# One hybrid decoder layer on one Trainium2 core: preparation behind the masks, fill between sample rounds, the inverse sent in pieces, and z loaded by ScalarE

## The chip, the cores and the metric

The kernel runs on one core of a Trainium2 chip. The metric is the time of one execution on the device in microseconds (us). The core has five engines with an instruction queue each: TensorE (PE, matrix products), VectorE (DVE), ScalarE (ACT), GpSimd (POOL) and SyncE (SP, which issues transfers only). Matrix products land in PSUM, a small memory of banks. SBUF is the large on-chip memory.

## The reference

One layer of a decoder is computed for a prompt of 512 tokens and for 8 sample requests of 4 tokens each, which share the weights; so T = 544 columns go through every product.

```python
def trunk_layer(x, wkv0, shift0, conv0, p):
    x = layer_norm(ALPHA * x + 0.5 * swiglu(x, p["ffn1_wg"], p["ffn1_wu"], p["ffn1_wd"]), ...)
    proj = x @ p["w_in"]
    ...            # r, k, v, decay w, gate a, g from proj with a token shift
    o, wkv_new = wkv7_recurrence(r_h, w_h, k_h, v_h, kk, a_h, wkv0)
    ...            # group norm of o, bonus, gate g
    u = c_c * c_h  # short gated convolution of width 3
    z = cw[0] * u_full[:, 0:T] + cw[1] * u_full[:, 1:T+1] + cw[2] * u_full[:, 2:T+2]
    y_conv = c_b * z
    mix = jnp.concatenate([y_rwkv, y_conv], axis=-1) @ p["w_out"]
    x = layer_norm(ALPHA * x + mix, ...)
    x = layer_norm(ALPHA * x + 0.5 * swiglu(x, p["ffn2_wg"], p["ffn2_wu"], p["ffn2_wd"]), ...)

# wkv7_recurrence, one step per token and head (64 x 64 state S):
    sa = S @ (-kk)
    S = S * w[None, :] + outer(sa, kk * a) + outer(v, k)
    o = S @ r
```

The widths are 1024 for the model, 2816 for the FFN, 8 heads of 64, and 512 channels of convolution. All is in float32.

## The kernel before, in words

**Products.** A float32 product is made of three passes: weights and inputs are split into a high and a low part (`hl`, `xhl`, `hhl`), ACT writing the high part and DVE the low one (`wsplit`), and `mm3` issues high x high, high x low and low x high for each block of 128 x 128. A weight is loaded into a buffer of the ring `raw` by SP, split into one of the ring `hl`, and used. The two FFNs (`Ffn`, `pairs` for gate and up, `downs` for down) use a scheme with fewer block products; `pairs` keeps sums of partial products in `cpb`, `downs` also uses `cpb` as the staging buffer from which a transfer on POOL's queue adds into `z` (`z<-cpb`).

**PSUM.** Two rings: `big()` gives a bank named `mm` out of 3, `sm()` one named `sm` out of 5.

**Mixer.** Between the FFNs stands the mixer. The recurrence is computed in chunks of 64 tokens for 4 pairs of heads. Each `Pair` has the steps `gates`, `square`, `decays`, `prep` (all elementwise on DVE and ACT, with a small product) and `scores`. `scores` multiplies the prepared keys `bkb` with `AO` (`masked`: 8 chunks of the prompt and one for the samples), DVE masks the products into `SC`, the diagonal blocks go to DRAM (`Ad`), POOL scales `bkb`, and TensorE transposes values and keys into `UV` and `BK`. `own_a` and `own_b` interleave the projections of the next pair with its preparation.

**Fill.** What is independent, above all the convolution's projections (`convs`, three of them per convolution block, in halves of 24 products), stands in a queue `bg`. `take(n)` issues steps of 6 matmuls from it until n estimated ns are used; `scores`, `elim` and `sample` are generators whose yields say how much fill is to be put there. Where `pinned` is set TensorE keeps the program's order; elsewhere, and on the other engines, a scheduler orders the instructions. Every engine then runs its queue in order.

**Samples, inverse, chain.** `sample` computes the sample requests' tokens in three rounds of tiny products (each `X,D` and `AR,S`), while `elim` inverts 32 x 32 blocks on DVE in 31 steps (`tm`, `De`), sends them through DRAM (`Ad` to `AT`; `De`, `AT` to `Dd`; `Dd` to `DM`, `XT`) and combines them to 64 x 64 on TensorE. `chain` then goes through the 8 chunks: `values` (product, ACT copies W), `solve` (W with XT, copies UV on DVE and ACT), `reads`, `update`, `outputs`. While it runs, the convolution's result `ycd` is loaded into `xhl`, and the layer's input `xsp` into `z`, for the output product with `wo_c` and `wo_r`.

Of the kernel before, what the change touches and what calls it, by code (L numbers as in the profile page):

```python
# [62 lines left out]
def body(ctx: ExitStack, tc: tile.TileContext, xT, gu1, wd1, win, wo_c, wo_r, gu2, wd2, lora, vec, cst,  # L63
# [94 lines left out]

    def mm3(out, hl, src, ks, c0, c1, off=0, start=True, stop=True):
        n = len(ks)  # L160
        for i, k in enumerate(ks):
# [737 lines left out]
    class Pair:
# [61 lines left out]
        def scores(self):  # L961
            p, bkb, vf = self.p, self.bkb, vfs[self.p]
            def masked(a0c, n):
                qs = (sm(), sm())
# [4 lines left out]
                for par, q in enumerate(qs):  # L969
                    DVE.tensor_tensor(SC[:, p, par, a0c:a0c + n, :], q[:, :P * n].rearrange("p (c t) -> p c t", c=n),  # L970
                                      (msk if n > 1 else msks)[:, None, :].to_broadcast([P, n, P]), op=OP.mult)
# [524 lines left out]
```

## Time and profile before

| what | us |
|---|---|
| median of 3 runs | 1078.86 |
| lowest and highest run | 1077.85, 1079.99 |
| the profiled execution's own time | 1078.24 |
| its span, first to last instruction | 1076.4 |
| TensorE busy | 1052.9 |
| DVE, ACT, POOL busy | 833.4, 564.8, 206.2 |
| mean granted clock of TensorE | 0.993 |

The rows of the profile carry line numbers of the kernel before; a row like `PE sm L76 <- DVE hl L148: 2.3, 1, 2.3` says that TensorE's instructions of line 76 that write a bank `sm` waited for DVE's instruction of line 148 that writes `hl`, 2.3 us in all, once, at most 2.3. All matmuls have line 76, since one helper records them. A timeline row gives start, duration, engine, line, operation, output and input, the count, and in brackets the idle time before it with what ended it. `SPq` rows are transfers being issued by SP, not their movement. Rows of windows give for each engine busy us and count, then TensorE's granted clock, the DMA engines' busy share, and GB/s.

### The profile page before, as it was taken

Reading aid. Unit: us, or ns where it says so; the run is one execution under the profiler, and the core shown is the slowest. Engines: PE = TensorE matmul, PEld = TensorE weight load, DVE = VectorE, ACT = ScalarE, POOL = GpSimd, SP = SyncE. Lnnn points to the kernel's source line nnn. Section 1 sums busy time; section 2 is a strip of 40 time slices with the busy share of each in tenths; the row PEclk is TensorE's granted clock in tenths of the full one; section 3 lists DMA queues with packets and bytes.
Section 4 is the critical chain, followed back from the end, with each engine's and each line's share of the span. In section 5 each row is a group of like instructions: output and inputs, shape, how many; then the busy total and the mean of one; then the engine's idle time right before and its main releaser. Section 6 shows DMA issues by size and latency. Waiting matters only on the chain.

```text
span 1076.4 us, 22064 instructions
## 1 busy us (share of the span) xinstructions
PE 1052.9 (98%) x8960; PEld 1020.0 (95%) x8960; DVE 833.4 (77%) x1529; ACT 564.8 (52%) x1016; POOL 206.2 (19%) x296
## 2 busy tenths in 40 slices
PE   9999999999999999999999999999999999999996
PEld 8999999999999998898989889999999999999995
DVE  7788878888876767767588577788889798887655
ACT  6655555465553567556322454466555646555514
POOL 0122121312200024334311410001312122031000
PEclk9999999999999999999989999999999999999999
DMA  8558595775945130312515730243957759496302
GB/s 285 139 121 185 126 207 148 162 177 120 217 107 168 59 123 33 88 51 89 149 64 187 248 107 26 95 116 77 214 144 160 187 123 220 119 189 158 108 1 84
DMA packets 82903, 144.78 MB, mean 135 GB/s; under 512 B 20464, under 2 KB 44400, under 8 KB 82544
## 3 DMA queue, kind: packets, MB, share of 16 engines
q1 hardware_dynamic: 55600, 107.19, 30.8%
q0 software_dynamic: 27200, 36.18, 21.8%
q8 instruction: 70, 1.15, 0.4%
q14 instruction: 33, 0.27, 0.1%
HBM read 124.37 MB, written 10.06 MB: 125 GB/s over the span
## 4 chain that ended last, share of the span: by engine, by line
PE 81%; DVE 9%; DMA 4%; ACT 3%; issue 3%; SPq 0%; ACTq 0%; DVEq 0%; POOL 0%; POOLq 0%
PE mm L76 52%; PE sm L76 29%; DMA z<-cpb 2%; DVE hl L148 2%; DMA raw<-in_gu 1%; ACT hl L147 1%; DVE SC L970 1%; DVE hhl L152 1%; DVE De L1023 1%; DVE tm L1021 1%; DMA z<-in_xT 1%; DVE z L623 1%; DMA raw<-in_win 0%; DMA ycd<-zc 0%; SPq L711 0%
## 5 line engine op out<-in xcount | busy, mean ns | idle before, releaser
L76 PE MATMUL mm<-xhl,hl 128*128 128x288 f32 (+2 forms) x2640 | 364.3, 294 | 3.3 <-DVE hl L148 2.3
L76 PEld LDWEIGHTS mm<-xhl,hl 128*128 128x128 f32 x2640 | 345.0, 190 | 10.9 <-DVE hl L148 2.5
L148 DVE TENSOR_TENSOR hl<-raw,hl 128x1024 fp32r<-128x1024 f32 (+3 forms) x224 | 262.1, 1174 | 66.8 <-ACT hl L147 65.6
L147 ACT ACTIVATE hl<-raw 128x1024 fp32r<-128x1024 f32 (+3 forms) x224 | 224.4, 1013 | 87.9 <-DVE raw L499 30.3
L76 PE MATMUL sm<-xhl,hl 128*128 128x272 f32 (+1 forms) x1392 | 194.5, 289 | 1.0 <-ACT xhl L151 0.4
L76 PEld LDWEIGHTS sm<-xhl,hl 128*128 128x128 f32 x1392 | 182.4, 189 | 2.3 <-DVE xhl L152 0.8
L76 PE MATMUL mm<-tv,hl 128*128 128x272 f32 x864 | 121.5, 289 | 1.9 <-ACT cpb L593 1.8
L76 PE MATMUL mm<-hhl,hl 128*128 128x272 f32 (+2 forms) x792 | 119.3, 294 | 0.0
L76 PEld LDWEIGHTS mm<-tv,hl 128*128 128x128 f32 x864 | 113.4, 188 | 3.2 <-ACT cpb L593 2.9
L76 PEld LDWEIGHTS mm<-hhl,hl 128*128 128x128 f32 x792 | 106.0, 188 | 4.8 <-ACT sv L639 1.5
L76 PE MATMUL sm<-hhl,hl 128*128 128x272 f32 (+2 forms) x792 | 109.7, 288 | 0.0
L76 PEld LDWEIGHTS sm<-hhl,hl 128*128 128x128 f32 x792 | 103.0, 188 | 0.5
L505 POOL DMA_DIRECT2D raw<-in_gu x36 | 43.5, 1209 | 254.6 <-DVE cpb L595 78.9
L511 POOL DMA_DIRECT2D raw<-in_wd x32 | 39.3, 1469 | 269.1 <-DVE hlb L152 234.6
L76 PE MATMUL mm<-tv,hlb 128*128 128x272 f32 x432 | 61.1, 291 | 0.0
L76 PEld LDWEIGHTS mm<-tv,hlb 128*128 128x128 f32 x432 | 56.4, 188 | 1.5 <-ACT cpb L602 1.4
L151 ACT ACTIVATE hhl<-hk 128x272 fp32r<-128x272 f32 (+1 forms) x56 | 29.5, 526 | 37.6 <-DVE hk L569 16.6
L152 DVE TENSOR_TENSOR hlb<-raw,hlb 128x512 fp32r<-128x512 f32 x52 | 35.7, 686 | 5.1 <-ACT hlb L151 5.1
L219 ACT ACTIVATE lnq<-z 128x512 f32<-128x512 f32 (+1 forms) x24 | 15.1, 656 | 46.5 <-DVE z L218 46.4
L152 DVE TENSOR_TENSOR hhl<-hk,hhl 128x272 fp32r<-128x272 f32 (+1 forms) x56 | 31.3, 558 | 7.0 <-ACT hhl L151 6.9
L499 DVE TENSOR_TENSOR raw<-raw 128x512 f32<-128x512 f32 x52 | 35.8, 688 | 1.0
L76 PE MATMUL mm<-hhl,hlb 128*128 128x272 f32 (+2 forms) x264 | 36.4, 288 | 0.0
(294 smaller groups left out, 1306.1 us busy)
## 6 DMA issues: line engine op xcount, KB each, us to landing
raw<-in_gu SPq DMA_DIRECT2D x84, 512.0 KB, 4.6
raw<-in_gu POOLq DMA_DIRECT2D x36, 512.0 KB, 6.2
raw<-in_wd SPq DMA_DIRECT2D x32, 512.0 KB, 4.5
raw<-in_win SPq DMA_DIRECT2D x26, 512.0 KB, 3.6
raw<-in_wd POOLq DMA_DIRECT2D x32, 256.0 KB, 6.0
raw<-in_wd SPq DMA_DIRECT2D x16, 384.0 KB, 3.1
z<-cpb POOLq DMA_DIRECT2D x16, 272.0 KB, 9.4
z<-sv POOLq DMA_DIRECT2D x16, 272.0 KB, 6.8
```

What stands on the lines that cost most here:

```text
L76: ins = f(*args, **kw)
L147: ACT.activation(hl[:, 0, a:b], raw[:, a:b], AF.Copy)
L148: DVE.tensor_tensor(hl[:, 1, a:b], raw[:, a:b], hl[:, 0, a:b].bitcast(F32), op=OP.subtract)
L151: ACT.activation(hi, x, AF.Copy)
L152: DVE.tensor_tensor(lo, x, hi.bitcast(F32), op=OP.subtract)
L219: squares.append(ACT.activation(qq, zz, AF.Square))
L499: DVE.tensor_tensor(y[:, :, 0], y[:, :, 1], a[:, :, 1], op=OP.add)
L505: POOL.dma_start(x.rearrange("p (s c) -> p s c", s=2), bass.AP(tensor=a11.tensor, offset=a11.offset, ap=[[2 * D, P], [P * 2 * D, 2], [1, 5 ...
L511: POOL.dma_start(four(x)[:, i], bass.AP(tensor=a11.tensor, offset=a11.offset, ap=[[DFF, P], [P * DFF, 2], [1, 256]]), accum_op=OP.add)
L623: hold(DVE.tensor_tensor(z[:, d, lo], z[:, d, lo], o, op=op))
L970: DVE.tensor_tensor(SC[:, p, par, a0c:a0c + n, :], q[:, :P * n].rearrange("p (c t) -> p c t", c=n), (msk if n > 1 else msks)[:, None, :].t ...
L1021: DVE.tensor_tensor(tv, AT[:, k, k + 1:32, None].to_broadcast([P, n, k + 1]), De[:, k, None, 0:k + 1].to_broadcast([P, n, k + 1]), op=OP.mult)
```

## The change

- `FILL` for `p0` and `p3` goes from 2500 to 1900 (three steps of fill instead of four) and is left out after pair 0; before pair 0's last projections half a convolution projection (24 matmuls) is issued; weights 4 to 6 are fetched earlier.
- The next pair's `square` stands behind the last matmul of its projections, and its `prep` behind the masks of the pair before (`mk`).
- `scores`: the single chunk takes one bank of each ring; POOL scales in two groups of 4 chunks; `Ad` gets the 32 x 32 blocks alone, in four transfers instead of two; the transposes go in groups of 4 and 5 instead of 5 and 4, with fill between.
- `Ffn.pairs`: the partial sums lie elsewhere in `cpb` for even u.
- The convolution's `zc` has two buffers.
- `elim`: `Ad` and `Dd` are laid out so that AT is read in rows of 4 KB; rows 0 to 23 of De are sent after step 22, the rest after step 30, each with its own loads of DM.
- `sample`: fill of 1400 between the rounds; copies that DVE made are made by ACT; buffers share names.
- `chain`: the first values of both groups are computed before the inverse's last part; ACT issues the four loads of z within the chain, where SP issued them ahead of it.

How this moves the instructions is read from their order in the built programs. The first place is TensorE's order where pair 0 has been prepared, just before its last projections (`kq,cs` is the norm of its keys, `T,cpb` a gate's product, `xhl,hl` a projection or fill). Before:

```order
L76 MATMUL sm<-kq,cs 128x256
L76 MATMUL sm<-kq,cs 128x320
L76 MATMUL mm<-xhl,hl 128x256 x24
L76 MATMUL mm<-xhl,hl 128x288 x24
L76 MATMUL sm<-T_4315,cpb 128x256 x2
```

And now:

```order
L76 MATMUL sm<-kq,cs 128x256
L76 MATMUL sm<-kq,cs 128x320
L76 MATMUL mm<-xhl,hl 128x288 x24
L76 MATMUL mm<-xhl,hl 128x256 x24
L76 MATMUL mm<-xhl,hl 128x288 x24
L76 MATMUL sm<-T_4315,cpb 128x256 x2
```

The 24 matmuls of half a convolution projection have come ahead of the two halves of the projection.

The second place is TensorE's order through the samples (`AR,S` reads the state, `X,D` or `X,WT` is a round's small product, `xhl,hl` is fill, `SI,SC` follows the rounds). Before:

```order
L76 MATMUL sm<-cs,SC 32x32 x8
L76 MATMUL sm<-AR_4716,S_6282 64x2x4 x16
L76 MATMUL sm<-X_6287,D_6286 32x32 x8
L76 MATMUL sm<-AR_4716,S_6282 64x2x4 x16
L76 MATMUL sm<-X_6287,D_6286 32x32 x8
L76 MATMUL sm<-AR_4716,S_6282 64x2x4 x32
L76 MATMUL mm<-xhl,hl 128x288 x18
L76 MATMUL sm<-SI,SC 64x64 x8
L76 MATMUL mm<-xhl,hl 128x256 x12
L76 MATMUL sm<-W,X_6287 64x64 x8
```

And now:

```order
L76 MATMUL sm<-cs,SC 32x32 x8
L76 MATMUL sm<-AR_4716,S_6300 64x2x4 x16
L76 MATMUL mm<-xhl,hl 128x288 x12
L76 MATMUL mm<-xhl,hl 128x256 x6
L76 MATMUL sm<-X_6304,WT 32x32 x8
L76 MATMUL sm<-AR_4716,S_6300 64x2x4 x16
L76 MATMUL mm<-xhl,hl 128x256 x18
L76 MATMUL sm<-X_6304,WT 32x32 x8
L76 MATMUL sm<-AR_4716,S_6300 64x2x4 x16
L76 MATMUL mm<-xhl,hl 128x288 x12
L76 MATMUL sm<-AR_4716,S_6300 64x2x4 x16
L76 MATMUL mm<-xhl,hl 128x288 x12
```

12 or 18 fill matmuls now stand behind each of the rounds' products.

The third place is ACT's order at the chain (W and UV are the chain's copies, one of each for the two groups in every step; `hl<-raw` is a weight split; `z<-xsp` the load of z). Before, from the copies of XT on:

```order
L147 ACTIVATE hl<-raw 128x1024
L839 ACTIVATE cu<-zc 128x544
L1051 COPY XT<-sm 32x16x32 x2
L1081 ACTIVATE W_7211<-sm 128x128
L1081 ACTIVATE W_7218<-sm 128x128
L1099 COPY UV<-sm 64x2x64 x2
L1081 ACTIVATE W_7263<-sm 128x128
L1081 ACTIVATE W_7277<-sm 128x128
L1099 COPY UV<-sm 64x2x64 x2
L1081 ACTIVATE W_7329<-sm 128x128
L1081 ACTIVATE W_7343<-sm 128x128
```

And now, from the second step (c=1) on:

```order
L1376 DMA z<-xsp 128x1088
L1094 ACTIVATE W_7287<-sm 128x128
L1112 COPY UV<-sm 64x2x64
L1376 DMA z<-xsp 128x1088
L1112 COPY UV<-sm 64x2x64
L1376 DMA z<-xsp 128x1088
L1094 ACTIVATE W_7339<-sm 128x128
L1094 ACTIVATE W_7353<-sm 128x128
L1376 DMA z<-xsp 128x1088
L1112 COPY UV<-sm 64x2x64 x2
L147 ACTIVATE hl<-raw 128x1024
L1094 ACTIVATE W_7406<-sm 128x128
```

The four loads of z and a weight split of `wo_c` stand among the copies; a second split stands two rows on, between the UV copies of c=3. DVE's halves of both splits have moved in the same way.

On SP, z's loads were issued between `xhl` and the first load of `wo_r`; now two loads of `wo_c` stand there:

```order
L130 DMA raw<-in_wo_c 128x1024
L1369 DMA xhl<-ycd 128x4x544 x2
L130 DMA raw<-in_wo_c 128x1024 x2
L130 DMA raw<-in_wo_r 128x1024
L1128 DMA out_wkvp<-W_7720 128x128
```

The second of the two splits is of the weight whose load stands right behind `xhl`.

The diff, without context that repeats and without edits that only rename:

```diff
-FILL = dict(l1a=1.754, l1b=0.752, p0=2500, s=600, p3=2500, e0=1.0, e1=1.0, g0=1.0, g1=1.0, l2a=1.5, l2b=1.4, l3a=1.35)
+FILL = dict(l1a=1.754, l1b=0.752, p0=1900, s=600, p3=1900, e0=1.0, e1=1.0, g0=1.0, g1=1.0, l2a=1.5, l2b=1.4, l3a=1.35)
...
+    last = [None]
+
     def mm3(out, hl, src, ks, c0, c1, off=0, start=True, stop=True):
...
             PE.matmul(out, wh, src[:, 1, k, c0:c1], start=False, stop=False)
-            PE.matmul(out, wl, src[:, 0, k, c0:c1], start=False, stop=(stop and i == n - 1))
+            last[0] = PE.matmul(out, wl, src[:, 0, k, c0:c1], start=False, stop=(stop and i == n - 1))
             if i % 2 and not (stop and i == n - 1):
...
-            def tail(u, b1, b3, cp):
+            def tail(u, b1, b3, cp, c2):
...
             for u in range(m1 - m0):
-                a = 0 if u % 2 else 3 * TB
-                cp = cpb[:, a:a + 3 * TB]
+                a = 0 if u % 2 else 4 * TB
+                cp, c2 = cpb[:, a:a + 2 * TB], cpb[:, (2 if u % 2 else 3) * TB:][:, :TB]
                 b1, b4, b3 = big()[:, :TB], sm()[:, :TB], sm()[:, :TB]
...
                 yield from prod(b1, u, "x", 0, tb(1), False)
-                self.copied = ACT.activation(cp[:, 2 * TB:], b1, AF.Copy)
+                self.copied = ACT.activation(c2, b1, AF.Copy)
                 hold(self.copied,
-                     DVE.tensor_tensor(cp[:, 2 * TB:], cp[:, 2 * TB:], b3, op=OP.add))
...
         u = cvp.tile([P, 2 + TP + 6 * NSEQ], F32, name="cu")
-        zc = cvp.tile([P, T], F32, name="zc")
+        zc = cvp.tile([P, T], F32, name="zc", bufs=2)
...
-    Ad = dr.tile([2, 32, 65, 64], F32, name="Ad")
-    Dd = [dr.tile([2, 32, 2, 32, 32], F32, name=f"Dd{i}") for i in range(2)]
+    Ad = dr.tile([2, 32, 2, 32, 32], F32, name="Ad")
+    Dd = [dr.tile([2, 32, *n, 32, 32], F32, name=f"Dd{i}") for i, n in enumerate(((), (2,)))]
...
             p, bkb, vf = self.p, self.bkb, vfs[self.p]
+            Pv = Pe[:, p, :, None, None]
+
             def masked(a0c, n):
-                qs = (sm(), sm())
+                qs = (sm(), sm() if n > 1 else big())
                 for c in range(n):
...
                 for par, q in enumerate(qs):
-                    DVE.tensor_tensor(SC[:, p, par, a0c:a0c + n, :], q[:, :P * n].rearrange("p (c t) -> p c t", c=n),
+                    self.mk = DVE.tensor_tensor(SC[:, p, par, a0c:a0c + n, :], q[:, :P * n].rearrange("p (c t) -> p c t", c=n),
                                       (msk if n > 1 else msks)[:, None, :].to_broadcast([P, n, P]), op=OP.mult)
-            masked(0, 4)
-            masked(4, 4)
+            for c in (0, 4):
+                masked(c, 4)
+                POOL.tensor_tensor(bkb[:, c:c + 4], bkb[:, c:c + 4], Pv[:, c:c + 4].to_broadcast([P, 4, 2, 64]), op=OP.mult)
             for par in range(2):
-                dma(Ad[par].rearrange("(c d) s t -> d s c t", d=4)[p, 0:64], SC[R(par), p, par, 0:8, 0:64])
-            POOL.tensor_tensor(bkb[:, 0:8], bkb[:, 0:8], Pe[:, p, :, None, None].to_broadcast([P, 8, 2, 64]), op=OP.mult)
+                for b in range(2):
+                    dma(Ad[par, :, b].rearrange("(c d) s t -> d s c t", d=4)[p],
+                        SC[64 * par + 32 * b:64 * par + 32 * b + 32, p, par, 0:8, 32 * b:32 * b + 32])
             yield 1
             masked(8, 1)
-            for a0c, n in ((0, 5), (5, 4)):
+            for a0c, n in ((0, 4), (4, 5)):
                 qs = (big(), sm())
...
                     PE.transpose(qs[1][R(0), d], vf[R(1), t:t + 64], ident[R(1), :])
+                if a0c == 0:
+                    yield 1
                 for par, q in enumerate(qs):
...
         tm = ep.tile([P, 256], F32, name="tm")
-        dma(AT, bass.AP(tensor=Ad.tensor, offset=Ad.offset, ap=[[2080, P], [64, 32], [1, 32]]))
+        dma(AT, Ad.rearrange("a c b s t -> (a c b) s t"))
         POOL.memset(De, 0.0)
...
             DVE.tensor_tensor(De[:, k + 1:32, 0:k + 1], De[:, k + 1:32, 0:k + 1], tv, op=OP.add)
+            if k in (22, 30):
+                a, b = (0, 24) if k == 22 else (24, 32)
+                dma(Dd[0].rearrange("a c s t -> (a c) s t")[:, a:b], De[0:P:2, a:b])
+                for par in range(2):
+                    dma(DM[64 * par + a:64 * par + b].rearrange("p c d t -> p (c d) t"),
+                        Dd[0][par, :, a:b].rearrange("c s t -> s c t"))
             yield 550
         DVE.tensor_copy(AT, De.rearrange("p a b -> p b a"))
-        for d, x in zip(Dd, (De, AT)):
-            dma(d.rearrange("a c b s t -> (a c b) s t"), x)
+        dma(Dd[1].rearrange("a c b s t -> (a c b) s t"), AT)
         B = lambda par, b: slice(64 * par + 32 * b, 64 * par + 32 * b + 32)
-        for i, (x, b) in enumerate(((DM, 0), (XT, 1), (XT, 0))):
+        for b in (1, 0):
             for par in range(2):
-                dma(x[B(par, b)].rearrange("p c d t -> p (c d) t")[:, :, 32 * b:32 * b + 32],
-                    Dd[i > 0][par, :, b].rearrange("c s t -> s c t"))
+                dma(XT[B(par, b)].rearrange("p c d t -> p (c d) t")[:, :, 32 * b:32 * b + 32],
+                    Dd[1][par, :, b].rearrange("c s t -> s c t"))
         est.close()
...
                 PE.matmul(q[R(par), pl * 64:pl * 64 + 64], SC[r, p, par, c, 0:64], UV[r, p, par, c, :], start=True, stop=True)
-            W[g] = tl([P, 2, 64], F32, name=f"W{g}")
+            W[g] = tl([P, 2, 64], F32, name=f"W{g}") if c else AR8[:, g]
             ACT.activation(W[g], v2(q), AF.Copy)
...
+        values(0, 0)
+        values(1, 0)
+        yield 0
         for c in range(8):
...
                 qo[:] = big(), big()
-            values(0, c)
             if c:
+                values(0, c)
                 reads(0, c)
-            values(1, c)
+                values(1, c)
             solve(0, c)
...
                 else:
-                    (ACT.copy if par else DVE.tensor_copy)(D8[r], qv)
+                    ACT.copy(D8[r], qv)
             reads(rnd)
-            yield 0
+            yield 1400
         reads(3)
         for par in range(2):
...
             POOL.memset(SC[pr, :, par, 8, HC[1 - par]], 0.0)
-            (ACT.copy if par else DVE.tensor_copy)(SC[pr, :, par, 8, HC[par]], sv[par][pr, :, 0, :])
-            (ACT.copy if par else DVE.tensor_copy)(WT[pr], sv[par][pr, :, 1, :])
+            ACT.copy(SC[pr, :, par, 8, HC[par]], sv[par][pr, :, 0, :])
+            ACT.copy(WT[pr], sv[par][pr, :, 1, :])
         yield 1500
...
             PE.matmul(q[R(par), pl * 64:pl * 64 + 64], SC[:, pl, par, 8, 0:64], SI[:, pl, par, :], start=True, stop=True)
...
-        DVE.tensor_copy(UV[R(0), :, 0, 8, :], v4(q[0], R(0)))
-        ACT.copy(UV[R(1), :, 1, 8, :], v4(q[1], R(1)))
+        for par in range(2):
+            ACT.copy(UV[R(par), :, par, 8, :], v4(q[par], R(par)))
...
         yield from project(i + 1, p, 0, rf)
-        yield from act(pairs[p].square)
         yield from project(i + 1, p, 1, rf)
+        with tc.issue_after(last[0].ins):
+            pairs[p].square()
         pairs[p].done = 1
...
         yield from act(pairs[p].decays)
-        yield from act(pairs[p].prep)
+        with tc.issue_after(pairs[p - 1].mk.ins):
+            pairs[p].prep()
+        yield 0
         yield from seq(*(project(4 + 3 * p, 8 + p, h, vfs[p]) for h in range(2)))
...
     ACT.activation(sgd, sgd, AF.Sigmoid)
+    wget(4)
+    wget(5)
     pairs[0].gates()
     pairs[0].square()
-    wget(4)
-    wget(5)
     pairs[0].decays()
     pairs[0].prep()
+    drain(islice(convs, 4))
+    wget(6)
     drain(project(4, 8, 0, vfs[0]), project(4, 8, 1, vfs[0]))
...
             need(p + 1, 2)
-            take(FILL["p0"])
+            if p:
+                take(FILL["p0"])
     pst.close()
...
     drain(conv3)
+    cpool = [None]
+    ch = chain(XT, lambda *a, **k: cpool[0].tile(*a, **k))
+    next(ch)
     for _ in el:
...
     z = pool(ctx, "zp2", "right").tile([P, KD, T], F32, name="z")
-    for k in range(0, KD, 2):
-        dma(z[:, k:k + 2, :], xsp[:, k:k + 2, :])
     cst0 = ExitStack()
-    cp = pool(cst0, "chain")
-    for _ in chain(XT, cp.tile):
-        pass
+    cpool[0] = pool(cst0, "chain")
+    for i, _ in enumerate(ch):
+        if i % 4 == 1:
+            k = i // 2
+            ACT.dma_start(z[:, k:k + 2, :], xsp[:, k:k + 2, :])
     pinned[0] = False
```

More of the change, by code (lines that the diff above doesn't have):

```diff
@@ L556, in tail @@
                 if i == 0:
-                    hold(ACT.activation(s[:, 1, hi], cp[:, 2 * TB:], AF.Silu, scale=-1.0))
+                    hold(ACT.activation(s[:, 1, hi], c2, AF.Silu, scale=-1.0))
                 else:
-                    DVE.scalar_tensor_tensor(s[:, 1, hi], cp[:, 2 * TB:], -1.0, s[:, 1, hi], op0=OP.mult, op1=OP.mult)
+                    DVE.scalar_tensor_tensor(s[:, 1, hi], c2, -1.0, s[:, 1, hi], op0=OP.mult, op1=OP.mult)
                     hold(DVE.tensor_tensor(s[:, 0, lo], s[:, 0, lo], cp[:, 0:TB], op=OP.mult))
@@ L601, in pairs @@
                 yield from prod(b1, u, "x", 0, tb(1), False)
-                self.copied = ACT.activation(cp[:, 2 * TB:], b1, AF.Copy)
+                self.copied = ACT.activation(c2, b1, AF.Copy)
                 hold(self.copied,
-                     DVE.tensor_tensor(cp[:, 2 * TB:], cp[:, 2 * TB:], b3, op=OP.add))
-                old = tail(u, b1, b3, cp)
+                     DVE.tensor_tensor(c2, c2, b3, op=OP.add))
+                old = tail(u, b1, b3, cp, c2)
             yield from old
@@ L1145, in sample @@
         dma(S0, s0)
-        WT = tl([P, 4, 32], F32, name="WT")
         SI = tl([P, 4, 2, 64], F32, name="SI")
-        D8 = tl([P, 4, 32], F32, name="D8")
+        D8 = tl([P, 4, 32], F32, name="WT")
         X8 = tl([P, 4, 64], F32, name="X8")
-        UP = tl([P, 4, 64], F32, name="UP")
         HR = [slice(96 * par, 96 * par + 32) for par in range(2)]
@@ L1182, in sample @@
                 else:
-                    (ACT.copy if par else DVE.tensor_copy)(D8[r], qv)
+                    ACT.copy(D8[r], qv)
             reads(rnd)
-            yield 0
+            yield 1400
         reads(3)
+        WT = tl([P, 4, 32], F32, name="WT")
         for par in range(2):
@@ L1195, in sample @@
             PE.matmul(q[R(par), pl * 64:pl * 64 + 64], SC[:, pl, par, 8, 0:64], SI[:, pl, par, :], start=True, stop=True)
-        W = tl([P, 4, 64], F32, name="W")
+        W = tl([P, 4, 64], F32, name="UP")
         ACT.activation(W, v4(q), AF.Copy)
@@ L1201, in sample @@
             PE.matmul(q[par][R(par), pl * 64:pl * 64 + 64], X8[R(par), pl, :], W[R(par), pl, :], start=True, stop=True)
-        DVE.tensor_copy(UV[R(0), :, 0, 8, :], v4(q[0], R(0)))
-        ACT.copy(UV[R(1), :, 1, 8, :], v4(q[1], R(1)))
+        for par in range(2):
+            ACT.copy(UV[R(par), :, par, 8, :], v4(q[par], R(par)))
+        UP = tl([P, 4, 64], F32, name="UP")
         DVE.tensor_tensor(UP, UV[:, :, 0, 8, :], UV[:, :, 1, 8, :], op=OP.add)
```

## The prediction

> **What bounds the kernel now.** I read the page's busy shares first, then TensorE's waits, then the granted clock by window, then the timeline at the places where either shows a loss.
>
> ```profile
> span 1076.4 us, 22064 instructions
> PE 1052.9 (98%) x8960; PEld 1020.0 (95%) x8960; DVE 833.4 (77%) x1529; ACT 564.8 (52%) x1016; POOL 206.2 (19%) x296
> ```
> TensorE is busy for 98% of the span, and the change neither adds nor removes a matmul. So it can win only TensorE's idle time (23.5 us in all, 1076.4 less 1052.9, much of it outside the stretch that is touched) and stretches at half clock. Of the first, this is what the waits show in the stretch that is touched (us in total, times, longest):
>
> ```profile
> PE sm L76 <- DVE SC L970: 2.4, 8, 0.4
> PE mm L76 <- DVE hl L148: 2.3, 1, 2.3
> PE mm L76 <- ACT cpb L593: 1.8, 2, 1.4
> PE sm L76 <- ACT W L1081: 1.1, 1, 1.1
> PE mm L76 <- ACT zc L853: 1.0, 1, 1.0
> PE sm L76 <- ACT BK L999: 0.8, 1, 0.8
> ```
> Of the second, the windows show two stretches at half clock (PEclk is the granted share):
>
> ```profile
> 425.97:429.38 3.41, 3.11 (x14) 3.11 (x15) 2.73 (x6) 2.53 (x5) 2.27 (x8) 0.50 0.42 154
> 545.44:552.27 6.83, 6.83 (x61) 6.41 (x57) 3.21 (x11) 1.39 (x3) 0.00 (x0) 0.50 0.00 0
> 601.00:627.00 26.00, 24.54 (x606) 22.21 (x608) 13.69 (x48) 9.30 (x33) 11.17 (x28) 1.00 0.63 228
> ```
> The third row is the chain of chunk steps; it keeps the full clock though its matmuls are small.
>
> **The change, part by part.**
>
> *FFN, -1.8.* In both FFNs the first copy of a pass wrote bytes of `cpb` that the accumulating transfer `z<-cpb` was still reading. Its waits:
> ```profile
>   DMA z<-cpb: 3.6, 5
> ```
> TensorE felt 1.8 of these 3.6 us. The new layout puts the first copy in a part of `cpb` that this transfer doesn't read, and the piece that does overlap is written four products later. Bounds 0 and -1.9; I take the row.
>
> *Pair 0 start, -3.6.* TensorE waits once for a weight split while DVE works through pair 0's preparation, and then runs at half clock:
> ```profile
> 426.27 4.25 PE L76 MATMUL mm<-xhl,hl 128*128 128x256 f32 x22 [2.33 <-DVE hl L148]
> 430.36 0.86 PE L76 MATMUL sm<-kq,cs 128*128 128x256 f32 x3
> ```
> The change puts 24 fill matmuls ahead of this and the splits earlier on DVE. At the 7.82/60 = 0.130 us a matmul of the dense stretch quoted below, they cover 3.1 us, more than the 2.33 waited. The half clock: 24 matmuls (22 recorded) took 430.36 - 426.27 = 4.09 instead of 3.12, so about -1.0; half of 3.41 us is the upper bound, -1.7. I take -1.3 since the window opens before 426.27. If another split is late instead, the wait returns with it: bounds 0 and -4.0.
>
> The Trainium skill, "TensorE: Matmul & The Clock Gate", Part 1, says that the clock drops after at least one idle window of about 3.4 us and that the windows run freely. Here 2.33 us of idling sufficed, and the sample rounds below lost the clock with a busy TensorE, so the trace does not bear out an entirely idle window. By the rule, closing 2.33 us would leave these 1.3 us where they are and the sum 1.3 poorer.
>
> *Pair scores, -2.9.* The single-chunk mask now uses a buffer of the other PSUM ring, preparation stands behind the masks on DVE, pair fill is put between the two groups of transposes, and POOL scales in halves. These are the 2.4 (eight waits, two a pair) and 0.8 above, 3.2 together. Preparation behind masks makes the next pair's `bkb` later by what it is moved past, about 2 us. For the last pair:
> ```profile
> 514.89 0.75 DVE L958 TENSOR_TENSOR bkb<-kq,Pn 64x576 f32<-64x576 f32 x1
> 524.63 1.61 PE L76 MATMUL sm<-AO,bkb 64*128 64x128 f32 x24
> ```
> `bkb` is done at 515.6 and wanted at 524.6: 9 us cover it, and without that cover it would cost the 2. I leave 0.1 a pair for what is late next. Bounds 0 and -3.2. The shorter `take`s only move fill steps; the first pair gives up what it took ahead of time.
>
> *Sample rounds, -3.1.* Three rounds of tiny matmuls run back to back, and the clock falls:
> ```profile
> 544.13 2.53 PE L76 MATMUL sm<-AR,S 64*64 64x8 f32 x64
> 546.59 4.69 PE L76 MATMUL mm<-xhl,hl 128*128 128x288 f32 x18
> 551.20 1.12 PE L76 MATMUL sm<-SI,SC 128*64 128x64 f32 x16
> 552.26 1.68 PE L76 MATMUL mm<-xhl,hl 128*128 128x256 f32 x12
> 553.86 0.68 PE L76 MATMUL sm<-W,X 64*64 64x64 f32 x16
> ...
> 585.50 7.88 PE L76 MATMUL mm<-xhl,hl 128*128 128x288 f32 x60 [1.00 <-ACT zc L853]
> 593.32 2.21 PE L76 MATMUL sm<-DM,SC 32*32 32x32 f32 x128
> ```
> 18 dense matmuls took 551.20 - 546.59 = 4.61 instead of 18 x 0.130 = 2.34 (2.27 lost); the 16 of SI,SC took 1.06, those of W,X 0.62 (0.44 lost); the AR,S before, some 0.4. Half of 6.83 is the bound, 3.4. Twelve to 18 dense matmuls between all rounds should keep the clock, as the chain's 64-wide matmuls do. Bounds 0 and -3.4; I take 3.1. The four copies that go from DVE to ACT are covered by the same fill.
>
> *Second `zc` buffer, -1.0.* ACT's `zc` copy waited for the last one's store, and TensorE behind it (its row above):
> ```profile
> 585.07 0.69 ACT L853 ACTIVATE zc<-mm 128x256 f32<-128x256 f32 x2 [2.30 <-DMA ycd<-zc]
> ```
>
> *The inverse's transfers, 0.* They end on the path only if XT is later than TensorE:
> ```profile
> 584.23 0.19 DVE L1023 TENSOR_TENSOR De<-De,tm 128x31 f32<-128x31 f32 x1
> 584.45 1.05 DVE L1025 COPY AT<-De 128x1024 f32<-128x1024 f32 x1
> 589.20 4.54 SPq L1031 DMA_DIRECT2D XT<-Dd  x4
> XT<-Dd SPq DMA_DIRECT2D x4, 128.0 KB, 3.9
> ycd<-cu SPq DMA_DIRECT2D x3, 272.0 KB, 3.8
> ```
> XT's last load is issued at about 593.2 and lands near 597.1, just when TensorE wants it, so every microsecond that TensorE saves before must be saved here too. It should be: AT is read in long rows and lands sooner, four copies leave DVE, DM goes ahead in two pieces. New on SP: `ycd<-cu` stands behind `Dd<-AT`, and DVE's next `cu` waits for its landing, 585.5 + 3.8 = 589.3; TensorE needs that buffer back 48 matmuls into the row at 585.50, at 591.8. Hidden by 2.5 us. The twelve or so extra issues on SP (`Ad`, De, DM) cost SP alone, which is not on the path.
>
> *Chain's start, -0.5.* The first W is copied before XT is there; of 1.1 us waited, the copy of XT stays exposed for about half.
>
> *z issued by ACT, +1.2.* Four issues now stand in ACT's queue among the copies on which TensorE waits:
> ```profile
> 610.34 0.28 ACT L1081 ACTIVATE W<-sm 128x128 f32<-128x128 f32 x1 [1.25 <-PE sm L76]
> 611.11 0.28 ACT L1081 ACTIVATE W<-sm 128x128 f32<-128x128 f32 x1 [0.49 <-PE sm L76]
> 611.49 0.26 ACT L1099 COPY UV<-sm 64x128 f32<-64x128 f32 x1
> 612.00 0.26 ACT L1099 COPY UV<-sm 64x128 f32<-64x128 f32 x1 [0.25 <-PE sm L76]
> ...
> 602.85 1.26 SPq L1344 DMA_DIRECT2D xhl<-ycd  x2
> 604.20 3.30 SPq L1347 DMA_DIRECT2D z<-xsp  x4
> ```
> On SP they took 3.30 in all. ACT's own gaps at their four places (0.49, 0.25, none, none) take up about 0.7 to 2.1, and the first also waits for the last `ycd<-zc` store. Bounds +0.2 and +2.9.
>
> *Two weight splits fall into the chain, +3.0.* This is the part the change does not name. Two splits of wo_c stand in ACT's and DVE's order after the copies of c=2 and between the UV copies of c=3. The first fits ACT's gap of 1.25. The second costs 1.06 less a gap of 0.25, and it must wait for its load, issued at about 604.2 behind `xhl<-ycd`:
> ```profile
> 597.36 1.06 ACT L147 ACTIVATE hl<-raw 128x1024 fp32r<-128x1024 f32 x1 [1.18 <-PE mm L76]
> raw<-in_wo_c SPq DMA_DIRECT2D x1, 512.0 KB, 3.9
> raw<-in_wo_r SPq DMA_DIRECT2D x1, 512.0 KB, 13.2
> xhl<-ycd SPq DMA_DIRECT2D x2, 1088.0 KB, 9.0
> ```
> A load ahead of that traffic lands in 3.9 us (608.1), one behind it in 13.2 (617.4). Its place is nearer the second; I take 11, 615.2. ACT comes to it at 611.75 + 1.2 = about 613.0. So 2.2 + 0.8 = +3.0; bounds +0.4 and +5.2.
>
> The Trainium skill, "DMA: Bandwidth & Descriptors", "Issuing engines are not separate DMA queues", says that transfers from all engines interleave on the same 16 engines, and that a second issuer saves only issue time. That speaks against taking z from SP: z would then no longer stand behind this load, but share with it.
>
> *Sum:* -1.8 - 3.6 - 2.9 - 3.1 - 1.0 - 0.5 + 1.2 + 3.0 = -8.7. The profiled execution's own time was 1078.24 (1.84 around its span), 0.62 below the median 1078.86; 1078.86 - 8.7 = 1070.2, **1070 us**.
>
> **Rivals.** *The chain costs next to nothing* (the load lands before ACT comes, issues fit the gaps): +0.6 instead of +4.2, 1066.6. For it: TensorE's shift of ACT's arrival; against it the 13.2. *The chain pays in full:* +2.9 and +5.2, 1074.1. *The inverse becomes the bound:* DVE's steps are interleaved with convolution work that waits for TensorE, and if De ends no earlier, the 4.1 of sample and `zc` are lost at XT: 1074.3; against it the 2.5 us at the `cu` buffer and shorter transfers. *Half clock stays* at both places (rounds of tiny matmuls remain in each window): 4.4 lost, 1074.6. *Slower:* the second split's load shares with xhl's and z's 4.4 MB at the chain's mean 228 GB/s: 4.9 MB take 21.5 us, it lands at 625.7, ACT stands still for 12.7 us, and the kernel takes 1070.2 - 3.0 + 13.5 = 1080.7. It decides from a landing at about 624 on; against it, no load in the rows took over 13.2.
>
> **Numbers.** Forecast 0.42 (alone 1068 to 1072.5), cheap chain 0.22, chain in full 0.10, inverse 0.08, half clock 0.12, slower 0.06. A measurement of this kernel tells about 0.2%, 2.2 us, from no change. All but the last case lie beyond it; of two of the upper ones together I leave 0.03 for the same. The range 1065 to 1075.5 reaches from below the cheap chain to above the three dear cases. Faster 0.91, same 0.03, slower 0.06.
>
> **What would show it.** TensorE's waits for hl, SC, BK, zc and cpb gone; no window at half clock at pair 0 or the samples; DMA XT landed before TensorE comes; in the chain an ACT wait for `raw<-in_wo_c` at c=3 and TensorE idle of 2 to 4 us behind it. I am wrong if that wait is absent, or XT is waited for.

## The result and the profile after

The changed kernel takes 1072.49 us (median of six runs, 1070.5 to 1073.96), the kernel before 1078.36 beside it (six runs, 1075.59 to 1082.45): a ratio of 0.9941, 95% interval 0.9918 to 0.9964. It is faster by 5.9 us where 8.7 were forecast. The profiled execution took 1073.96, with a span of 1072.2; against the profiled one of before the span is shorter by 4.2, and the working below goes by that. It is the longest of the six, so the profile shows 1.5 us less of a gain than the medians do.

TensorE's waits in the changed kernel (us in total, times, longest):

```profile
PE sm L76 <- ACT UV L1112: 9.0, 1, 9.0
...
PE mm L76 <- ACT cpb L595: 0.8, 2, 0.5
PE sm L76 <- DVE X L1195: 0.6, 1, 0.6
```

The waits of before for `hl`, SC, BK, `zc` and W are gone from the list, that for `cpb` is halved. In their place stands one wait of 9.0 us for a copy of UV on ACT. The windows of the changed kernel at the places of before, with the granted clock behind the engines:

```profile
425.97:429.38 3.41, 3.41 (x30) 3.41 (x29) 2.10 (x4) 3.09 (x9) 2.38 (x8) 1.00 0.48 161
531.00:552.00 21.00, 20.45 (x310) 19.13 (x309) 19.17 (x44) 6.29 (x16) 2.20 (x3) 1.00 0.29 103
601.06:614.71 13.65, 6.38 (x102) 5.91 (x102) 3.49 (x9) 3.48 (x8) 1.42 (x4) 0.50 0.48 185
587.38:623.94 36.56, 27.15 (x608) 24.38 (x609) 16.29 (x49) 12.22 (x36) 12.04 (x28) 0.81 0.52 192
```

Both stretches at half clock of before are gone (rows 1 and 2), and a longer one has come in the chain (row 3). Row 4 is the chain from its first product to the first `AO,cs` behind it. The timelines of TensorE and of ACT show its loss:

```profile
599.01 0.28 PE L76 MATMUL sm<-UV,BK 128*64 128x64 f32 x2
608.33 0.58 PE L76 MATMUL sm<-UV,BK 128*64 128x64 f32 x5 [9.04 <-ACT UV L1112]
```

```profile
597.78 0.26 ACT L1112 COPY UV<-sm 64x128 f32<-64x128 f32 x1
606.94 1.06 ACT L147 ACTIVATE hl<-raw 128x1024 fp32r<-128x1024 f32 x1 [8.89 <-DMA raw<-in_wo_c]
608.02 0.26 ACT L1112 COPY UV<-sm 64x128 f32<-64x128 f32 x1
```

This is the wait that the prediction named: between the two UV copies of c=3 ACT stands for the load of a weight block that the chain does not need. TensorE needs the second copy and stands too. SP's queue shows when the load was issued, and the DMA rows of the stretch what went with it (KB each, median us from issue to landing):

```profile
589.25 1.27 SPq L1369 DMA_DIRECT2D xhl<-ycd  x2
590.57 0.83 SPq L130 DMA_DIRECT2D raw<-in_wo_c  x1
```

```profile
xhl<-ycd SPq DMA_DIRECT2D x2, 1088.0 KB, 13.6
z<-xsp ACTq DMA_DIRECT2D x4, 544.0 KB, 9.7
```

The 13.6 is the median of two transfers; a window around the second alone shows what it took:

```profile
xhl<-ycd SPq DMA_DIRECT2D x1, 1088.0 KB, 15.7
```

The load is issued at 590.57, ACT is ready for it at 598.04 and gets it at 606.94, 16.4 us after the issue (the landing itself is not in the profile).

**Where the 4.2 us came from.** I compare the times at which TensorE has done the same work; where fill has moved past such a point, the moved matmuls are counted at 0.130 us. Rows of before and of after that mark the points:

```profile
530.82 1.24 PE L76 MATMUL sm<-Pn,cs 128*128 128x256 f32 x4
...
593.32 2.21 PE L76 MATMUL sm<-DM,SC 32*32 32x32 f32 x128
...
627.18 0.70 PE L76 MATMUL sm<-AO,cs 128*128 128x256 f32 x2
```

```profile
432.80 1.13 PE L76 MATMUL sm<-kq,cs 128*128 128x256 f32 x4
521.38 1.24 PE L76 MATMUL sm<-Pn,cs 128*128 128x256 f32 x4
580.54 2.21 PE L76 MATMUL sm<-DM,SC 32*32 32x32 f32 x128
585.08 2.21 PE L76 MATMUL sm<-XT,DM 32*32 32x32 f32 x128
623.94 0.70 PE L76 MATMUL sm<-AO,cs 128*128 128x256 f32 x2
```

| part | forecast | measured | how |
|---|---|---|---|
| FFN up to pair 0 | -1.8 | 0 | its first product begins at 409.07 before, 409.11 after |
| pair 0 start | -3.6 | -3.8 | 432.80 - 430.36 = +2.44, less 48 more matmuls done by then (6.2) |
| the four pairs | -2.9 | -6.4 | last `Pn` -9.44 with 6 more matmuls done (0.8), less the 3.8 |
| sample rounds and `zc` | -4.1 | -2.6 | DM,SC -12.78, less the three rows above |
| inverse, start of chain | -0.5 | -1.1 | chain from 601.30 to 587.38, less -12.78 |
| the chain | +4.2 | +10.7 | 25.88 before, 36.56 after |
| behind the chain | 0 | -1.0 | rest of the span; the second FFN's share of the -1.8 would lie here |

Up to the chain 13.9 us were won (12.9 forecast). The chain gave 10.7 of them back.

### The profile page after: what moved, and what is told of

Read it like the earlier page. It is cut to its first block, busy times and chain, and to the rows that moved or that the text cites. A ratio compares the mean times of both kernels' runs of the same rounds, so it can differ in the third digit from the quotient of the medians.

```text
span 1072.2 us, 22082 instructions
## 1 busy us (share of the span) xinstructions
PE 1047.8 (98%) x8960; PEld 1017.0 (95%) x8960; DVE 832.6 (78%) x1525; ACT 565.0 (53%) x1020; POOL 205.3 (19%) x300
## 4 chain that ended last, share of the span: by engine, by line
PE 84%; DMA 6%; issue 5%; ACT 2%; DVE 2%; SPq 1%; ACTq 0%; POOL 0%; POOLq 0%; DVEq 0%
PE mm L76 54%; PE sm L76 29%; DMA raw<-in_gu 3%; DMA raw<-in_wo_c 2%; ACT hl L147 1%; DMA z<-in_xT 1%; DVE hl L148 1%; DMA AT<-Ad 1%; DMA raw<-in_wo_r 0%; SPq L713 0%; DVE tm L1029 0%; DVE De L1031 0%; ACT z L263 0%; DMA Ad<-SC 0%; ACT hlb L151 0%
## 5 line engine op out<-in xcount | busy, mean ns | idle before, releaser
L76 PE MATMUL mm<-xhl,hl 128*128 128x256 f32 (+2 forms) x2640 | 362.2, 293 | 0.0
```

The costliest lines, as they stand in the source:

```text
L76: ins = f(*args, **kw)
```

## The experiments

The theory after the result: ACT's order puts a weight split ahead of a copy that the chain needs, and its load is late because it stands behind `xhl<-ycd` on SP's queue, which is itself slow while z runs beside it. The rival is that the four z issues on ACT are dear in themselves. All ratios are to the kernel before, run in the same comparison.

**e1_z_sp: z on SP again, right behind `xhl`.**
```
-        if i % 4 == 1:
-            k = i // 2
-            ACT.dma_start(z[:, k:k + 2, :], xsp[:, k:k + 2, :])
...
+    for k in range(0, KD, 2):
+        dma(z[:, k:k + 2, :], xsp[:, k:k + 2, :])
```


> The changed kernel with one part undone: z is loaded by SP again, right behind xhl. In its order the second split of wo_c then stands at c=7 of the chain instead of c=3. Theory A (the chain's loss is ACT standing at that split, 8.9 us, for a load queued behind xhl, and the half clock after it, 2.3 us): no ACT wait for raw in the chain, chain 25 to 26.5 us from the first AR,XT to the first AO,cs instead of 36.6, time about 1072.5 - 11 = 1061 (1059.5 to 1063). Rival B (the four issues on ACT and the traffic are the loss, whoever issues z, and the split only shows it): z ahead of the weight makes its load later still, time 1070 to 1074.

1063.49 us, 0.9863 (0.9842 to 0.9884): 9.0 faster than the changed kernel, and 0.5 above the range of theory A. The chain in its profile, and the DMA rows:
```profile
585.80:613.26 27.46, 25.04 (x608) 22.25 (x609) 16.42 (x50) 12.37 (x36) 12.91 (x28) 1.00 0.65 240
```
```profile
xhl<-ycd SPq DMA_DIRECT2D x2, 1088.0 KB, 8.3
z<-xsp SPq DMA_DIRECT2D x4, 544.0 KB, 10.0
```
No wait for `raw`, full clock, and `xhl` lands in 8.3 instead of 15.7 (the second transfer of each; the first's landing is not in e1's profile). But the edit also moved the second split to c=7, so it does not tell whether the issues, the traffic or the split's place cost the 9 us.

**e2_hold: z stays on ACT, the two late splits go behind the chain's last copies.**
```
-    wc = [wload(wo_c[i]) for i in range(4)]
+    wc = []
+    for i in range(4):
...
+        with ExitStack() as held:
+            if i > 1:
+                for t in tails:
+                    held.enter_context(tc.issue_after(t.ins))
+            wsplit(hl, raw, 0, 1024)
...
```


> The changed kernel with z on ACT kept, but the splits of the third and fourth part of wo_c ordered behind the chain's last copies on ACT and DVE. Theory A: the 9.0 us wait and the half clock go, time 1061 to 1062, within 1 us of the kernel with z on SP, since four issues cost ACT little (+0.2 to +1.2). Rival B: z on ACT costs by itself, 2.9 us or more over the kernel with z on SP: 1064 or more. A loss of its own: the held splits are late after the chain, a TensorE wait for hl at about 611 to 616, up to 2 us.

(`tails` are the chain's last copies.) 1064.35 us, 0.9872 (0.985 to 0.9894). That is above the range of theory A, and it meets the 1064 of rival B; but rival B asked for 2.9 us over e1, and it is 0.9. With the issues on ACT kept and only the splits moved, nearly all is back: the issues are not the cost.

**e5_zlate: z is issued by ACT behind c=3.**
```
-        if i % 4 == 1:
-            k = i // 2
-            ACT.dma_start(z[:, k:k + 2, :], xsp[:, k:k + 2, :])
+        if i >= 8 and i % 2 == 0:
+            k = i - 8
+            with tc.issue_after(tails[0].ins):
+                ACT.dma_start(z[:, k:k + 2, :], xsp[:, k:k + 2, :])
```


> The changed kernel with z's four issues on ACT moved behind c=3 (c=4 to c=6). The second split then stands at c=6. Theory A: no wait for raw, time 1061 to 1062.5. It also tells what made that load late: the load behind xhl alone, without z's 2.2 MB beside it, should land 9 to 11 us after its issue if sharing with z was the cause of the 16.3 us, and still 14 us or more if standing behind xhl was. A new risk: z itself lands late for the output product, 1 to 3 us of TensorE wait after the chain.

(`tails[0]` is here the copy of the outputs at c=3.) 1064.19 us, 0.9875 (0.9843 to 0.9907), the median of 1061.84, 1062.09, 1066.30 and 1068.23. The two longer executions had a mean clock of 0.994 and 0.992, the shorter ones 0.998 and 0.997; the profile is of the shortest and does not show what the longer ones lost. In it the split stands at c=6 and waits for nothing, but its load still goes right behind `xhl`, now without z beside it. A window around its issue gives that load alone:
```profile
xhl<-ycd SPq DMA_DIRECT2D x2, 1088.0 KB, 9.6
raw<-in_wo_c SPq DMA_DIRECT2D x1, 512.0 KB, 10.7
```
So the load takes 10.7 us behind `xhl` alone, and 16.4 with z's four transfers on the other queue.

**e11_rawfirst: z on ACT, splits in the chain, `xhl` behind the load.**
```
-    for j in range(2):
-        dma(xhl[:, j, 4:8].bitcast(F32), ycd[:, :, j])
...
+        d = dma(raw, wo_c[i])
+        ld = d if i == 2 else ld
...
+    with tc.issue_after(ld.ins):
+        for j in range(2):
+            dma(xhl[:, j, 4:8].bitcast(F32), ycd[:, :, j])
```


> The changed kernel, z still on ACT, both splits still in the chain; only the two transfers xhl<-ycd are put behind the load that the second split waits for. Theory A (that load is late because it stands behind xhl on SP's queue, and z's traffic stretches xhl): it lands 4 to 7 us after its issue, ACT waits for it less than 1.5 us, no half clock, time 1062 to 1065. Rival (z's traffic beside it makes it late wherever it stands): it lands 10 us or more after its issue, a wait of 4 us or more stays, 1067 or more.

1063.52 us, 0.985 (0.9826 to 0.9874). Both splits stand in the chain, and ACT does not wait for them; the load's row of the same profile below:
```profile
594.28 2.00 ACT L147 ACTIVATE hl<-raw 128x1024 fp32r<-128x1024 f32 x2
```
```profile
raw<-in_wo_c SPq DMA_DIRECT2D x3, 512.0 KB, 4.7
xhl<-ycd SPq DMA_DIRECT2D x2, 1088.0 KB, 12.6
z<-xsp ACTq DMA_DIRECT2D x4, 544.0 KB, 10.0
```
This settles the place of the loss. z on ACT and splits in the chain together cost no more than z on SP (1063.52 and 1063.49), once the load does not stand behind `xhl`. `xhl` itself takes 12.6 here and nobody waits for it.

**e3_nofill: the changed kernel without the fill between the sample rounds.**
```
-            yield 1400
+            yield 0
```


> The changed kernel without the fill between the three sample rounds (0 instead of 1400). The prediction's term: the half clock of 6.8 us is back at the samples and costs 3.1, time 1075.6 (1074.5 to 1076.5). Rival: the fill is worth less than that, since the trace shows 2.6 us won from the samples to the inverse with the zc buffer's 1.0 in it, so 1.5: 1074.

1076.63 us, 0.9982 (0.9967 to 0.9997), 4.1 slower than the changed kernel. The half clock is back; the first row is the stretch ahead of it:
```profile
530.76:534.17 3.41, 3.32 (x100) 2.95 (x99) 3.27 (x10) 0.51 (x2) 0.00 (x0) 1.00 0.41 156
534.17:544.41 10.24, 9.44 (x109) 8.99 (x111) 5.98 (x17) 2.45 (x6) 0.00 (x0) 0.50 0.01 2
```
TensorE is busy for 3.32 of 3.41 us ahead of the fall and for 9.44 of the 10.24 behind it. DM,SC comes 3.55 us later by the trace, net of the 0.35 by which this execution reached the mixer earlier. The term of 3.1 holds. The profile is of the longest of ten executions; its chain is 1.8 us longer too.

The remaining parts were undone one at a time from e1, where the chain does not cover them up; e13 does one part alone from before. Where they ran in other comparisons than e1, I go by the difference of the ratios (1% is 10.8 us).

**e6_cpb: the old places in `cpb`.**
```
-                a = 0 if u % 2 else 4 * TB
-                cp, c2 = cpb[:, a:a + 2 * TB], cpb[:, (2 if u % 2 else 3) * TB:][:, :TB]
+                a = 0 if u % 2 else 3 * TB
+                cp, c2 = cpb[:, a:a + 2 * TB], cpb[:, a + 2 * TB:a + 3 * TB]
```


> Base is the changed kernel with z on SP (1063.5), which has no stall in the chain. Undone on it: the places of the partial sums in cpb, in both FFNs. The prediction's term: the waits on cpb are back, 1.8, time 1065.3. Rival, by the traces after the change (first kq at 408.3 instead of 409.1, and 0.5 less in the second FFN): 1.0 to 1.3, since the wait moves to other copies: 1064.6.

1064.16 us, 0.9861 (0.9845 to 0.9877): not told from e1. TensorE's wait for `cpb` is 1.2 us in its trace, 0.9 in e1's: 0.3 of the 1.8. The times alone, with intervals of 0.2% on either side, do not exclude the 1.8. ACT's timelines before and after the change, at the longest of these waits, show why so little is won:
```profile
142.84 2.95 ACT L147 ACTIVATE hl<-raw 128x1024 fp32r<-128x1024 f32 x3 [0.76 <-DMA raw<-in_gu]
146.15 0.40 ACT L593 ACTIVATE cpb<-mm 128x272 f32<-128x272 f32 x1 [0.36 <-DMA z<-cpb]
```
```profile
143.18 2.96 ACT L147 ACTIVATE hl<-raw 128x1024 fp32r<-128x1024 f32 x3 [0.75 <-DMA raw<-in_gu]
146.04 0.37 ACT L595 ACTIVATE cpb<-mm 128x272 f32<-128x272 f32 x1
```
The copy stands behind the same three weight splits in both. TensorE waited 1.38 us for it before, but only 0.36 of that was for `z<-cpb`; it went on at 146.60 before and at 146.47 after.

**e7_scores: the old masks, POOL scaling at once, groups of five and four chunks without fill between them.**
```
-                qs = (sm(), sm() if n > 1 else big())
+                qs = (sm(), sm())
...
-            for a0c, n in ((0, 4), (4, 5)):
+            for a0c, n in ((0, 5), (5, 4)):
...
-                if a0c == 0:
-                    yield 1
```


> Same base. Undone: the two rings for the single-chunk mask, POOL's scaling in two groups, the groups of 4 and 5 with fill between. Preparation stays behind the masks. The prediction's term for all of the pair scores was 2.9, so at most +3.2 here: 1066.4. Rival: the traces show 6.5 won over the four pairs (2.3, 1.5, 1.6, 1.1); if fill between the groups is what won it, +5 to +6.5, 1069 to 1070, and TensorE's excess at each pair is 1.1 to 1.6 again.

1069.94 us, 0.9917 (0.9895 to 0.9939): 5.8 slower than e1 by ratio, yet at equal work the pairs lose only 1.8 of it. The rival's 1069 to 1070 came, but not for its reason. More is lost later, in the inverse. SP's queue and DVE there:
```profile
576.62 0.41 SPq L1038 DMA_DIRECT2D Dd<-AT  x1
577.07 0.46 SPq L843 DMA_DIRECT2D ycd<-cu  x1
```
```profile
581.66 0.75 DVE L858 TENSOR_TENSOR cu<-zc,mm 128x256 f32<-128x256 f32 x2 [6.38 <-DMA ycd<-cu]
```
Here the store of `cu` stands on SP behind `Dd<-AT`; DVE waits 6.38 us for its landing, TensorE 2.1 for DVE, and a half clock of 17.07 us follows from 583.28. This profile is of the longest of the four executions (1072.86, mean clock 0.989); the others took 1068.15 to 1070.14 at 0.996 and 0.997, so by their clocks they did not have that half clock. Of the 5.8 the trace accounts for 1.8 in the pairs and the 2.1 waited for DVE; the rest is open. It is the order that the prediction held hidden by 2.5 us. It is hidden in the changed kernel; 18 fill matmuls fewer in the pairs, 2.3 us, and it is on the path.

**e8_prep: `square` and `prep` again where they stood, not behind the masks.**
```
+        yield from act(pairs[p].square)
...
-        with tc.issue_after(last[0].ins):
-            pairs[p].square()
...
-        with tc.issue_after(pairs[p - 1].mk.ins):
-            pairs[p].prep()
-        yield 0
+        yield from act(pairs[p].prep)
```


> Same base. Undone: square behind the projections' last matmul and prep behind the masks. If the order on DVE is what won the unforeseen 3.6 us of the pairs: +2 to +4, 1065.5 to 1067.5, with DVE SC waits back. Prediction: with the second ring and the fill in place the masks' lateness is hidden, 0 to +1.

1068.1 us, 0.9898 (0.988 to 0.9916): 3.8 slower than e1 by ratio, 4.6 in the medians. TensorE's waits, and its last `Pn` (520.59 in e1):
```profile
PE sm L76 <- DVE SC L974: 2.1, 3, 1.0
...
PE sm L76 <- ACT kq L920: 1.1, 1, 1.1
```
```profile
525.71 1.24 PE L76 MATMUL sm<-Pn,cs 128*128 128x256 f32 x4
```
The masks are waited for again, so the prediction's 0 to +1 does not hold.

**e13_order_alone: the kernel before with only this order changed.**
```
+            last[0] = PE.matmul(out, wl, src[:, 0, k, c0:c1], start=False, stop=(stop and i == n - 1))
...
-        yield from act(pairs[p].square)
+        with tc.issue_after(last[0].ins):
+            pairs[p].square()
...
-        yield from act(pairs[p].prep)
+        with tc.issue_after(pairs[p - 1].mk.ins):
+            pairs[p].prep()
+        yield 0
```


> The kernel before with one part alone: square behind the projections' last matmul and prep behind the masks of the pair before. Undoing it on the changed kernel cost 4.6. If it is worth as much alone, the four pairs take 4 to 5 us less up to the last Pn and the time is 1074 to 1075 (against 1078.9). Prediction: it alone removes most of the 2.4 of DVE SC waits and nothing else, 1076.5.

1075.36 us against 1079.86 of before in the same comparison, 0.9962 (0.9942 to 0.9981): 4.1 us by this order alone. The windows and TensorE's timeline at pair 0:
```profile
425.97:429.38 3.41, 3.31 (x27) 3.31 (x28) 2.56 (x6) 2.66 (x7) 2.16 (x8) 1.00 0.43 154
```
```profile
426.07 6.06 PE L76 MATMUL mm<-xhl,hl 128*128 128x256 f32 x46 [2.32 <-DVE hl L148]
```
It waits 2.32 us for the split as before did (2.33), and yet keeps the full clock there. The last `Pn` comes at 525.74 (530.82 before, with the same fill done); about 1.3 of this is won at pair 0, where the clock is kept, in the one execution that was profiled. `square` and `prep` were moved together and not tested apart.

**e9_zc: one `zc` buffer.**
```
-        zc = cvp.tile([P, T], F32, name="zc", bufs=2)
+        zc = cvp.tile([P, T], F32, name="zc")
```


> Same base. Undone: the second zc buffer. The prediction's term: +1.0, ACT zc waiting for the store ycd<-zc, TensorE behind it, 1064.5. In its order two weights of wo_c are loaded ahead of xhl, so the chain may change too. Rival: with the store's wait back in the sample stretch, where the ACT copies of the samples now queue behind zc, +2 to +3.

1074.39 us, 0.9956 (0.994 to 0.9972): 10.0 slower than e1 by ratio, where the wait in before was 1.0. SP's queue, ACT, and the clock:
```profile
571.61 1.47 SPq L1036 DMA_DIRECT2D DM<-Dd  x2
573.41 2.43 SPq L1044 DMA_DIRECT2D XT<-Dd  x4
575.88 0.56 SPq L844 DMA_DIRECT2D ycd<-zc  x1
```
```profile
579.72 0.68 ACT L855 ACTIVATE zc<-mm 128x256 f32<-128x256 f32 x2 [9.60 <-DMA ycd<-zc]
```
```profile
576.08:586.32 10.24, 6.16 (x26) 6.16 (x27) 0.42 (x1) 0.68 (x2) 0.00 (x0) 0.50 0.65 155
```
With the inverse's transfers in their new places, the store of `zc` is issued at 575.88, behind all of them. ACT waits 9.60 us for it, TensorE 8.3, and the half clock follows. Both expected times, 1064.5 and +2 to +3, were far too low.

**e10_vals: the chain's first values behind the inverse's last part.**
```
-    next(ch)
     for _ in el:
...
+    next(ch)
```


> Same base. The first values of both groups are computed behind the inverse's last part again. The prediction's term: +0.5; the traces from before to after show 1.1 between DM,SC and the chain's first solve: +1.1. So 1064.0 to 1064.6, with a TensorE wait on ACT W of about 1.

1064.05 us, 0.9856 (0.9832 to 0.988): not told from e1; TensorE waits 0.4 us for the first AR, which the 0.5 of the prediction is about.

**e12_onepiece: De sent in one piece, behind step 30.**
```
-            if k in (22, 30):
-                a, b = (0, 24) if k == 22 else (24, 32)
+            if k == 30:
+                a, b = 0, 32
```


> Base is the changed kernel with z on SP (1063.5). De is sent in one piece after step 30, as it was, still in the new layout. The prediction costed the pieces at 0, hidden by some 2.5 to 4 us: 1063.5 to 1064.5. Rival: DM then lands behind TensorE's arrival, 2 to 4 us of wait before DM,SC and perhaps a half clock after it: 1066 to 1069.

1064.75 us, 0.9858 (0.9834 to 0.9881): not told from e1. The two pieces are worth nothing measurable, as forecast.

## Why the prediction was right, and where not

The direction, the range and the mechanism that would cost were right: an ACT wait for `raw<-in_wo_c` at c=3 with TensorE idle behind it. That the sum came near is luck: two terms were wrong in opposite directions, the chain by +6.5 and the pairs by -3.5.

**The two splits in the chain, +3.0: the failed step is the landing of the load.** I took 11 us from issue to landing, with 13.2 as the upper bound from a row of before; it was 16.4. ACT came 7.5 us after the issue, 8.8 by the prediction. The 11 is what the load takes behind `xhl` alone (10.7 in e5); what the sum left out is z beside them. The 13.2 is from a load that stood behind `xhl` and z with all of them on SP's queue. Issued by ACT, z ran beside `xhl` and stretched its second transfer from 8.3 (e1) to 15.7, and the load stands behind `xhl`. The 9.6 of `xhl` with z later (e5) says the same. The Trainium skill, "DMA: Bandwidth & Descriptors", "Issuing engines are not separate DMA queues", says that transfers of all engines share the same 16 engines; the runs agree (4.7 ahead, 10.7 behind `xhl`, 16.4 behind `xhl` with z beside it). The prediction quoted it as speaking against the edit, and carried it into its rival for a slower kernel but not into its bound. The second omission is the clock: the half clock behind the stall costs some 2.3 us more, since the step to the update of c=4 took 5.11 instead of 3.18 and the next 3.54. The stall's 9.0 and these 2.3 are slightly more than the 10.7 by which the chain grew.

Of the rivals, the one for a slower kernel had this mechanism (the load sharing with `xhl` and z) with ACT standing 12.7 us; it stood 8.89, between that and the forecast. It did not decide: the landing came 16.4 us after the issue and not 21.5, and the parts ahead of the chain gave 1.0 more than forecast. *Half clock stays* and *the inverse becomes the bound* did not come: the windows of row 1 and 2 are at 1.00, and XT,DM starts 4.54 behind DM,SC (585.08 - 580.54) with no wait in TensorE's list.

**z on ACT, +1.2:** about 0 by itself (e11 against e1; 0.9 by e2, within the intervals). Even in e11 the chain takes 26.93, about 1 us more than before; the splits' own work in it is the likeliest rest of the forecast's 4.2, but that was not separated.

**Pair scores, -2.9 within 0 and -3.2: mis-sized, -6.4.** The order of preparation on DVE, which the prediction costed only as a delay of 2 us behind 9 us of cover, is the larger part: 3.8 to 4.6 by e8, 4.1 by e13 alone; masks, banks and groups are 1.8 (e7). The step that failed is to take the waits of before in the list, 3.2, as the upper bound. TensorE from the `kq` that ends the row of pair 0 to the last `Pn`, before and after:
```profile
430.36:530.82 100.46, 97.05 (x868) 89.32 (x866) 72.15 (x131) 54.28 (x113) 37.21 (x74) 1.00 0.28 84
```
```profile
432.80:521.38 88.58, 88.58 (x827) 82.44 (x825) 70.69 (x129) 52.07 (x109) 34.76 (x75) 1.00 0.26 79
```
The stretch is 11.9 us shorter, 5.5 of it for 42 fill matmuls that went elsewhere. Of the 6.4 left, 3.4 were idle time and 3.0 were time in which TensorE counts as busy. All but 0.2 lies in the score products and transposes (`AR,bkb`, `cs,bkb`, `cs,vt`), which take 14.3 us from one start to the next before and 8.2 after.

**Pair 0, -3.6:** -3.8. But its 1.3 for the half clock do not come with the idle time every time: e13's profiled execution had the same idle time without it.

**Sample rounds, -3.1:** 3.5 by the trace of e3, 4.1 in the medians, which hold its longer chain too. With `zc`, only 2.6 of the 4.1 forecast came; 0.6 of the shortfall is the new wait for X on DVE.

**`zc`, -1.0:** cannot be read apart in the totals. As a part of this change it is worth 10 (e9, on the base of e1). That the new order on SP is what makes one buffer dear is read from SP's rows: before, the store went out ahead of the inverse's transfers (581.03, `Dd` from 584.45). I costed the edits one by one against the trace of before; these two belong together.

**The inverse's transfers, 0, and the chain's start, -0.5:** both hold (e12, e10). The margin of 2.5 us that the prediction gave them was small: e7 used it up.

**FFN, -1.8:** 0 by the trace's points, and not told from none by e6. Over the profiles, the first `kq` begins at 408.2 to 409.4 in the eleven kernels with the new places and at 408.6 to 409.1 in the three with the old ones; from the chain's end on, e6 takes 448.27 us and the changed kernel 448.26. I took TensorE's whole wait as removed, though the copy stands in ACT's order behind splits and only a part of the wait was for the transfer.

## What to carry to other kernels

When a load moves to another engine's queue, bound the landing of the transfers that stay behind on the first queue by rows in which both ran together; and look in each in-order engine for an instruction nobody needs soon that waits for such a load ahead of one that the critical engine needs. Four versions that mend only this (e1, e2, e5, e11) take 1063.5 to 1064.4 us, ratios of 0.985 to 0.9875 to before. Each is 8 to 9 us below the changed kernel, more than the 5.9 that the whole change brought. A list of waits by releaser is no upper bound for what a new order can win: 3.0 of the pairs' 6.4 stood in time that counts as busy. Cost edits that share one queue together, since the worth of one (a second buffer: 1 us before, 10 after) depends on the other.

## What the runs showed of the hardware

The clock does not follow idling closely. In the changed kernel it fell at 601.06, 1.8 us after TensorE's last matmul, and rose at 614.71, 6.4 us after work had resumed at 608.33. The stretches at half clock are 3.41, 6.83, 10.24, 13.65 and 17.07 us long, one to five times 3.41 (the first two in before, the others in e3 and e9, in the changed kernel and in e7), and the two of before begin 119.47 us apart (425.97 and 545.44), 35 times 3.413. The same 2.3 us of idling lost the clock in before and kept it in e13. The Trainium skill, "TensorE: Matmul & The Clock Gate", Part 1, says that the windows run freely; that agrees, while its idle window of about 3.4 us is not what before shows, where TensorE was still busy for 1.39 of the 3.41 us ahead of the fall. An estimate for e13: counted back 34 times 3.413 from its own fall at 541.40, one window ends at 425.35 and divides the idle time from 423.75 to 426.07, and in the 3.41 us up to there TensorE was busy for 1.81. Then where the windows happened to lie decided it; no run tests this. And in e3 it fell with TensorE busy for 3.32 of the 3.41 us ahead, in 64x8 and 32x32 matmuls for the most part. That their small size is the cause was not tested by itself.

Left open: gaps of 0.4 to 1.2 us in the chain for which TensorE's list gives no releaser ("issue"), in e1, e10 and e12 but not in before or in the changed kernel.
